# Two-operand work taken off GpSimdE in the first mixer, and half of the stacked keys of two mixers copied by DMA inside SBUF

## The chip, the cores and the metric

The kernel runs on one core of a Trainium2 chip. The metric is device time in microseconds, the median over runs of one whole execution; the time of a profiled execution is given beside it. Engines are named as in the profile: PE (TensorE), DVE (VectorE), ACT (ScalarE), POOL (GpSimdE), SP (SyncE, which issues the DMAs here).

## What is computed

The reference is one inference step of a four-layer trunk over 128 context tokens and 512 latent tokens of width 1024. Each layer has a token mixer, a residual with layer norm, and a squared-ReLU MLP of width 4096. The mixers are, in order, differential attention, neighbourhood attention, grouped-query attention and a Hyena long convolution. The change touches the first two. Of the first mixer it matters that each of its 8 heads has two score maps, and that keys and queries of latent tokens are rotated:

```
def attend(k, v):
    k1, k2 = jnp.split(k, 2, axis=-1)
    def block(qb):
        q1, q2 = jnp.split(qb, 2, axis=-1)
        p1 = softmax_f32(jnp.einsum("bqhd,bkhd->bhqk", q1, k1) * scale)
        p2 = softmax_f32(jnp.einsum("bqhd,bkhd->bhqk", q2, k2) * scale)
        return jnp.einsum("bhqk,bkhd->bqhd", (p1 - lam * p2).astype(v.dtype), v)
...
o = rms_norm(o, subln_g) * (1.0 - lam_init)
out = o.reshape(B, L, DA_HEADS * 2 * DA_DH) @ w_o
```

The second mixer has 16 heads of 64 dimensions, handled in 8 pairs, with a learned bias on a window of keys, no rotation and no head norm.

## The kernel before

All matrix products run with operands split into a high part (fp32r) and a low part (the rest), each product as three matmuls (`mm3`, lines 473 to 475). Weights come from HBM by SP into three raw buffers (line 421); ScalarE casts the high part (line 450) and VectorE subtracts for the low part (line 451) into five buffers, from which a unit of matmuls reads.

A mixer (`mixer_attn`) runs over 8 heads (or head pairs) `j`. For each, generators project queries and keys (`prep_q`, `prep_k`) and, for two heads at a time, values (`prep_v`). Their small later steps are closures in the list `stages`: in the first mixer the rotation (`rope`: four DMAs inside SBUF bring the partner rows into `sw`, line 1002; then `turn`, lines 1011 and 1012; then `rope_add`, line 1018), and in both mixers the stacking. `q_stack` writes, for each of the two halves of 64 rows, the high part of the query beside its low part; `k_stack` (lines 1030 to 1033) writes the high part of the key's 64 rows into both row halves of `hi`, and the low part into both row halves of `lo`, so that one matmul over 128 rows covers two products (`score_mm`, line 2001). Of `k_stack`'s four instructions two are ScalarE casts, one is a VectorE subtraction and one a GpSimdE subtraction.

Each head has five units: four blocks of 128 latent queries (`DaUnit`, `NaUnit`) and one of context queries (`CtxUnit`). `run_units` staggers them: scores of one unit, softmax of the one before, combination of the one before that (`da_combine`: two reciprocals, a factor, a scale of the second map on line 2110, a scale-and-add on line 2112), transposes (`transposed`, copies on lines 1055 and 1057), then the values (lines 2152 and 2193). A `Feeder` hands out projection steps between the units, so that the matmuls of head `j + 1` fill the waits of head `j`; `opening` runs what is left of them before a head's first scores. After the heads `o_turn` scales the first mixer's outputs by their norms (line 1112), transposes them and applies the gain.

The order of instructions on PE, DVE, ACT and SP is made by a scheduler from its own costs and priorities in program order; on GpSimdE the order is that of the program, by the line

```
with tc.manual_schedule(engines={mybir.EngineType.Pool}):
```

Every engine and SP's queue execute in order, and each instruction waits for its inputs.

Of the kernel before, what the change touches and what calls it, by code (L numbers as in the profile page):

```python
# [10 lines left out]
F32 = mybir.dt.float32  # L11
F32R = mybir.dt.float32r
I32 = mybir.dt.int32
AF = mybir.ActivationFunctionType
# [4 lines left out]
P = 128  # L19
# [5 lines left out]
NT = TOK // P  # L25
# [253 lines left out]
class Trunk:  # L279
# [725 lines left out]
    def rope(self, x, cs):  # L1005

        nc = self.nc
        sw = self.swapped(x, LAT)

        def turn():  # L1010
            nc.gpsimd.tensor_mul(sw, sw, cs[:, 1])
            nc.vector.tensor_mul(x, x, cs[:, 0])
            self.turned = sw

        return turn
# [10 lines left out]
    def k_stack(self, hi, lo, x, h):  # L1026

        nc = self.nc
        own, oth = slice(64 * h, 64 * h + 64), slice(64 - 64 * h, 128 - 64 * h)
        nc.scalar.copy(hi[own], x[own])  # L1030
        nc.vector.tensor_sub(lo[own], x[own], hi[own].bitcast(F32))
        nc.scalar.copy(hi[oth], x[own])
        nc.gpsimd.tensor_sub(lo[oth], x[own], hi[own].bitcast(F32))

    def split(self, hi, lo, x):
        self.nc.scalar.copy(hi, x)
        self.nc.vector.tensor_sub(lo, x, hi.bitcast(F32))
# [65 lines left out]
    def o_turn(self, o, gain, ss, norm):  # L1103

        nc = self.nc

        def root(js):
            self.rsqrt(norm[:, :, js], ss[:, :, js], 1.0 / 128)

        def scale(j):  # L1110
            ov = o[:, :, j]
            nc.gpsimd.tensor_mul(ov, ov, norm[:, :, j:j + 1].to_broadcast([P, NT, P]))

        def turn(j):
            for t0, n in ((0, 3), (3, 2)):
                ps = self.b1([P, 3, P], "ot")
                for t in range(n):
                    nc.tensor.transpose(ps[:, t], o[:, t0 + t, j], self.ident)
                nc.scalar.activation(o[:, t0:t0 + n, j], ps[:, 0:n], AF.Copy, scale=gain)

        out = []
        for j0, n in ((0, 2), (2, 2), (4, 2), (6, 1), (7, 1)):
            out.append((j0 + n, lambda js=slice(j0, j0 + n): root(js)))
            for j in range(j0, j0 + n):
                out += [(j0 + n, lambda j=j: scale(j)), (j0 + n, lambda j=j: turn(j))]
        return out
# [13 lines left out]
    def mixer_attn(self, l):  # L1140
        nc, tc, a = self.nc, self.tc, self.a
        da = l == 0
        nm = "da" if da else "na"
        with tc.tile_pool(name=f"at{l}", bufs=1) as scr:
            self.scr = scr
            if da:
                o = self.L(F32, f"o{l}").rearrange("p (t k f) -> p t k f", t=NT, k=KD)
                split = self.o_parts(lambda kh, t: o[:, t, 4 * kh:4 * kh + 4])
            else:
                o = self.L(F32, f"o{l}").rearrange("p (k t) -> p k t", k=KD)  # L1150
# [6 lines left out]
            if da:  # L1157
                room = scr.tile([P, 2, 2, LAT], F32R, name="qroom")
                cs = vv[:, 0, 6:10].rearrange("p (a c) f -> p a (c f)", a=2)
# [9 lines left out]
                norm = scr.tile([P, NT, 8], F32, name="norm")  # L1169
# [64 lines left out]
            def prep_k(j):  # L1234
                k = self.S(F32, "k32")
                kc = kc_room[:, j % 2]
                h = heads.setdefault(j, {})
                h["kc"] = kc
                h["ks"] = [[ksr[:, j % 2, i, s] for s in range(2)] for i in range(2)]
                nc.sync.dma_start(k[:, cut:cut + CTX], a[nm + "_ck"][j])  # L1240
                yield from self.project(nm, 2 * j + 1, ((kc, 0, CTX, None), (k[:, 0:cut], CTX, CTX + cut, None), (k[:, cut + CTX:], CTX + cut, TOK, None)))
                nc.sync.dma_start(self.o[nm + "_ks"][j], kc)
                if da:
                    stages.append(self.rope(k[:, 0:LAT], cs))

                def stack():
                    if da:
                        self.rope_add(k[:, 0:LAT])
                    for i in range(2):
                        self.k_stack(*h["ks"][i], k, i)  # L1250

                stages.append(stack)
                if not (da and j == 0):
                    next(ada, None)
                    yield 850
# [850 lines left out]
def da_combine(nc, e0, e1, m, neglam):  # L2106

    nc.vector.reciprocal(m[:, 4:6], m[:, 2:4])
    nc.vector.tensor_mul(m[:, 5:6], m[:, 5:6], neglam)
    nc.gpsimd.tensor_mul(e1, e1, m[:, 5:6].to_broadcast(list(e1.shape)))  # L2110
    yield
    nc.vector.scalar_tensor_tensor(out=e0, in0=e0, scalar=m[:, 4:5], in1=e1, op0=ALU.mult, op1=ALU.add)

# [6 lines left out]
class DaUnit(Unit):  # L2120
# [5 lines left out]
    def scores(self):  # L2126
        k, nc, hd = self.k, self.k.nc, self.heads[self.j]
        pss = []
        for h in range(2):
            ps = k.b2([P, 2, 512], "s")  # L2130
            self.score_mm(ps, hd, h, FULL)
            pss.append(ps)
        yield
        m = k.small(6, "m")
        es = []
        for h, ps in enumerate(pss):
            k.softmax_stats(ps[:, :, :HALF], m[:, h:h + 1])
            e = k.S(F32, "e")
            nc.scalar.activation(e.rearrange("p (a b) -> p a b", a=2), ps[:, :, :HALF], AF.Exp, bias=m[:, h:h + 1], scale=1.0, accum_out=m[:, 2 + h:3 + h])
            es.append(e)  # L2140
        yield
        yield from da_combine(nc, es[0], es[1], m, self.neglam)
        yield es[0]
# [12 lines left out]
class CtxUnit(Unit):  # L2156
# [5 lines left out]
    def scores(self):  # L2162
        k, nc, hd = self.k, self.k.nc, self.heads[self.j]
        ps = k.b1([P, 2, P], "sc")
        for h in range(2):
            nc.tensor.matmul(ps[:, h], hd["qc"][:, h * P:(h + 1) * P], hd["kc"], start=True, stop=True)
        yield
        m = k.small(6, "m")
        nc.vector.tensor_reduce(m[:, 0:2], ps, axis=AX.X, op=ALU.max, negate=True)
        e = k.S(F32, "e", 256).rearrange("p (a b) -> p a b", a=2)  # L2170
        rs = hd["rs"][:, 0] if "rs" in hd else None
        if rs is not None:
            nc.vector.tensor_mul(m[:, 0:2], m[:, 0:2], rs)
        for h in range(2):
            nc.scalar.activation(e[:, h], ps[:, h], AF.Exp, bias=m[:, h:h + 1], scale=1.0 if rs is None else rs[:, h:h + 1], accum_out=m[:, 2 + h:3 + h])
        yield
        if self.neglam is not None:
            yield from da_combine(nc, e[:, 0], e[:, 1], m, self.neglam)
        else:
            nc.vector.reciprocal(m[:, 4:6], m[:, 2:4])  # L2180
            nc.gpsimd.tensor_mul(e, e, m[:, 4:6].unsqueeze(2).to_broadcast([P, 2, P]))
            yield
        yield e
# [37 lines left out]
```

## Time and profile before

| | |
|---|---|
| Median of 3 runs | 3435.16 us (3433.51 to 3438.25) |
| Profiled execution | 3427.73 us |
| Its span | 3425.9 us |
| Granted TensorE clock, mean | 0.993 |
| PE busy | 3297.3 us (96%) |
| PE weight loads busy | 3166.2 us (92%) |
| DVE busy | 2559.7 us (75%) |
| ACT busy | 1511.8 us (44%) |
| POOL busy | 823.4 us (24%) |

The span runs from the first to the last instruction of the profiled execution. Busy shares are averages over the whole span. Matmuls overlap, and their ends are modelled, so that a busy PE can still have room. Times within the rows are microseconds from the span's start. The first mixer's heads lie between about 50 and 400 us, the second's between about 950 and 1220 us.

### The profile page before, as it was taken

What the parts mean: (1) busy time and instruction counts of PE and PEld (TensorE: products, weight loads), DVE (VectorE), ACT (ScalarE), POOL (GpSimd) and SP (SyncE); (2) the same over time, 40 slices, a digit from 0 to 9 for tenths busy, and PEclk for the clock granted to TensorE, in tenths of its full rate; (3) what the DMA queues carried; (4) which work ended last, traced back from release to release, by engine and by line L of the source; (5) the groups of instructions that cost most, each with busy time, mean ns of one, the idle gap of its engine ahead of it and who ended that gap; (6) DMA issues with size and microseconds to landing.
All of it is one profiled execution on the core that took longest, in us unless ns stands there. A gap on an engine that the chain in (4) does not pass through costs nothing.

```text
span 3425.9 us, 63752 instructions
## 1 busy us (share of the span) xinstructions
PE 3297.3 (96%) x25288; PEld 3166.2 (92%) x25288; DVE 2559.7 (75%) x4876; ACT 1511.8 (44%) x2704; POOL 823.4 (24%) x842
## 2 busy tenths in 40 slices
PE   8999899999999999999998999999999999999998
PEld 6878898999999999999997889999998998999998
DVE  4777888788586678778678878877859888845457
ACT  3555453343366654333345665333325334532322
POOL 0323213334234431123222011231321112100002
PEclk9999999999999999999999999999999999999999
DMA  7343135555332325545422112545533224322221
GB/s 275 125 129 107 66 126 162 171 163 182 95 126 79 104 73 173 186 159 196 162 73 64 31 54 99 185 160 179 168 101 121 80 83 159 107 76 75 92 75 50
DMA packets 157643, 418.96 MB, mean 122 GB/s; under 512 B 19550, under 2 KB 29414, under 8 KB 154270
## 3 DMA queue, kind: packets, MB, share of 16 engines
q1 hardware_dynamic: 157344, 414.88, 36.9%
q8 instruction: 199, 3.26, 0.4%
q14 instruction: 100, 0.82, 0.1%
HBM read 371.20 MB, written 34.05 MB: 118 GB/s over the span
## 4 chain that ended last, share of the span: by engine, by line
PE 58%; DVE 12%; issue 4%; ACT 2%; POOL 1%; DMA 1%; SPq 0%; DVEq 0%; POOLq 0%; ACTq 0%
PE w L473 14%; PE w L474 14%; PE w L475 14%; DVE hl L451 2%; PE pv L2048 1%; DVE gtmp L653 1%; PE s L2001 1%; DVE ada L541 1%; PE ptp L1051 1%; PE qk L473 1%; PE qk L475 1%; PE qk L474 1%; PE py L1764 1%; DVE r L660 1%; POOL hywork L1742 1%
## 5 line engine op out<-in xcount | busy, mean ns | idle before, releaser
L451 DVE TENSOR_TENSOR hl<-raw,hl 128x1024 fp32r<-128x1024 f32 x411 | 537.7, 1311 | 319.5 <-ACT hl L450 318.4
L450 ACT CAST hl<-raw 128x1024 fp32r<-128x1024 f32 x411 | 430.2, 1048 | 674.9 <-PE w L475 552.0
L473 PE MATMUL w<-hl,ff 128*128 128x256 f32 x2560 | 715.8, 280 | 6.9 <-DVE gtmp L653 6.6
L474 PE MATMUL w<-hl,ff 128*128 128x256 f32 x2560 | 715.4, 279 | 2.0 <-DVE hl L451 1.9
L475 PE MATMUL w<-hl,ff 128*128 128x256 f32 x2560 | 713.9, 279 | 0.0
L660 POOL TENSOR_TENSOR r<-r,gtmp 128x256 f32<-128x256 f32 x416 | 413.5, 1007 | 1185.3 <-DVE gtmp L653 1135.9
L473 PE MATMUL w<-hh,hl 128*128 128x320 f32 (+2 forms) x2048 | 635.5, 310 | 2.7 <-ACT fx L875 2.3
L474 PE MATMUL w<-hl,hl 128*128 128x320 f32 (+2 forms) x2048 | 631.9, 309 | 3.3 <-DVE hl L742 3.3
L475 PE MATMUL w<-hh,hl 128*128 128x320 f32 (+2 forms) x2048 | 631.9, 309 | 0.0
L473 PEld LDWEIGHTS w<-hl,ff 128*128 128x128 f32 x2560 | 481.0, 188 | 11.2 <-DVE gtmp L653 9.3
L474 PEld LDWEIGHTS w<-hl,ff 128*128 128x128 f32 x2560 | 481.2, 188 | 4.5 <-DVE hl L451 2.8
L475 PEld LDWEIGHTS w<-hl,ff 128*128 128x128 f32 x2560 | 479.9, 187 | 0.0
L653 DVE TENSOR_TENSOR gtmp<-w,gate 128x256 f32<-128x256 f32 x800 | 326.3, 416 | 182.1 <-PE w L475 167.8
L541 DVE SCALAR_TENSOR_TENSOR ada<-adaw,sil,ada 128x512 f32<-128x512 f32 x504 | 388.1, 802 | 91.0 <-DMA adaw<-in_ada_w 80.9
L473 PEld LDWEIGHTS w<-hh,hl 128*128 128x128 f32 x2048 | 384.2, 188 | 17.6 <-issue 8.4
L474 PEld LDWEIGHTS w<-hl,hl 128*128 128x128 f32 x2048 | 384.3, 188 | 4.1 <-DVE hl L742 4.1
L475 PEld LDWEIGHTS w<-hh,hl 128*128 128x128 f32 x2048 | 384.1, 188 | 0.8 <-issue 0.8
L875 ACT ACTIVATE fx<-w 128x640 f32<-128x640 f32 (+2 forms) x136 | 91.5, 673 | 461.2 <-PE w L475 450.6
L473 PE MATMUL qk<-hh,hl 128*128 128x320 f32 (+2 forms) x672 | 215.2, 320 | 0.8 <-DVE gtmp L653 0.5
L474 PE MATMUL qk<-hl,hl 128*128 128x320 f32 (+2 forms) x672 | 210.8, 314 | 1.7 <-DVE hl L742 1.7
L475 PE MATMUL qk<-hh,hl 128*128 128x320 f32 (+2 forms) x672 | 210.4, 313 | 0.0
L473 PE MATMUL w<-hl,oh 128*128 128x256 f32 x640 | 184.0, 288 | 9.8 <-DVE gtmp L653 5.5
(340 smaller groups left out, 6810.6 us busy)
## 6 DMA issues: line engine op xcount, KB each, us to landing
raw<-in_w SPq DMA_DIRECT2D x256, 512.0 KB
adaw<-in_ada_w SPq DMA_DIRECT2D x288, 256.0 KB
adaw<-in_ada_w SPq DMA_DIRECT2D x16, 1024.0 KB
raw<-ab_d SPq DMA_DIRECT2D x32, 512.0 KB
raw<-in_hy_in SPq DMA_DIRECT2D x24, 512.0 KB
adaw<-in_ada_s SPq DMA_DIRECT2D x8, 1024.0 KB
raw<-in_da_qk SPq DMA_DIRECT2D x16, 512.0 KB
gate<-gate_d SPq DMA_DIRECT2D x32, 256.0 KB
```

The source lines that it names most:

```text
L450: self.nc.scalar.copy(t[:, 0], raw)
L451: self.nc.vector.tensor_sub(t[:, 1], raw, t[:, 0].bitcast(F32))
L473: mm(ps, w[0], x[0], start=start, stop=False)
L474: mm(ps, w[0], x[1], start=False, stop=False)
L475: mm(ps, w[1], x[0], start=False, stop=stop)
L541: nc.vector.scalar_tensor_tensor(out=y, in0=raw[h], scalar=x, in1=y, op0=ALU.mult, op1=ALU.add)
L653: nc.vector.tensor_mul(tmp, ps, self.gate[2 * s + q // 2][:, (q % 2) * 256:(q % 2) * 256 + 256])
L660: eng.tensor_add(rv, rv, tmp)
L875: nc.scalar.activation(x, src, AF.Relu)
L1051: nc.tensor.transpose(ps[:, i * P:(i + 1) * P], pr[:, (done + i) * P:(done + i + 1) * P], self.ident)
L1742: eng.tensor_mul(pi[:, q, s], z4[:, q, s], h4[:, q, 1 - s])
L1764: mm(py[ct][:, par], yh[:, i, cc], inv[h][:, kt, s, par], start=kt == 0 and i == 0 and h == 0, stop=False)
```

## The change

In the first mixer the rotation's second multiplication goes from GpSimdE to VectorE, behind the first; the scale of the second score map and the scale of the outputs by their norms go from GpSimdE to ScalarE, which takes the factor as a per-row operand (for the outputs one instruction for each of five token tiles, in place of one for all five). In the first two mixers a new function `k_stack_copied` takes the place of `k_stack`: ScalarE and VectorE write one row half of `hi` and `lo`, and two DMAs on SP copy each to the other row half inside SBUF. The third mixer keeps `k_stack`.

```
--- before.py
+++ after.py
@@ -1008,8 +1008,8 @@
         sw = self.swapped(x, LAT)
 
         def turn():
-            nc.gpsimd.tensor_mul(sw, sw, cs[:, 1])
             nc.vector.tensor_mul(x, x, cs[:, 0])
+            nc.vector.tensor_mul(sw, sw, cs[:, 1])
             self.turned = sw
 
         return turn
@@ -1031,6 +1031,15 @@
         nc.vector.tensor_sub(lo[own], x[own], hi[own].bitcast(F32))
         nc.scalar.copy(hi[oth], x[own])
         nc.gpsimd.tensor_sub(lo[oth], x[own], hi[own].bitcast(F32))
+
+    def k_stack_copied(self, hi, lo, x, h):
+
+        nc = self.nc
+        own, oth = slice(64 * h, 64 * h + 64), slice(64 - 64 * h, 128 - 64 * h)
+        nc.scalar.copy(hi[own], x[own])
+        nc.vector.tensor_sub(lo[own], x[own], hi[own].bitcast(F32))
+        for t in (hi, lo):
+            nc.sync.dma_start(t[oth].bitcast(F32), t[own].bitcast(F32))
 
     def split(self, hi, lo, x):
         self.nc.scalar.copy(hi, x)
@@ -1108,8 +1117,8 @@
             self.rsqrt(norm[:, :, js], ss[:, :, js], 1.0 / 128)
 
         def scale(j):
-            ov = o[:, :, j]
-            nc.gpsimd.tensor_mul(ov, ov, norm[:, :, j:j + 1].to_broadcast([P, NT, P]))
+            for t in range(NT):
+                nc.scalar.activation(o[:, t, j], o[:, t, j], AF.Copy, scale=norm[:, t, j:j + 1])
 
         def turn(j):
             for t0, n in ((0, 3), (3, 2)):
@@ -1247,7 +1256,7 @@
                     if da:
                         self.rope_add(k[:, 0:LAT])
                     for i in range(2):
-                        self.k_stack(*h["ks"][i], k, i)
+                        self.k_stack_copied(*h["ks"][i], k, i)
 
                 stages.append(stack)
                 if not (da and j == 0):
@@ -2107,7 +2116,7 @@
 
     nc.vector.reciprocal(m[:, 4:6], m[:, 2:4])
     nc.vector.tensor_mul(m[:, 5:6], m[:, 5:6], neglam)
-    nc.gpsimd.tensor_mul(e1, e1, m[:, 5:6].to_broadcast(list(e1.shape)))
+    nc.scalar.activation(e1, e1, AF.Copy, scale=m[:, 5:6])
     yield
     nc.vector.scalar_tensor_tensor(out=e0, in0=e0, scalar=m[:, 4:5], in1=e1, op0=ALU.mult, op1=ALU.add)
```

## Rows read from the trace of the kernel before

**Rows 1.** busy us of each engine in two stretches; then granted clock, DMA

```profile
50.00:400.00 350.00, 320.41 (x2291) 283.19 (x2291) 259.85 (x479) 188.88 (x455) 110.97 (x79) 0.98 0.38 123
950.00:1220.00 270.00, 263.95 (x2106) 252.41 (x2105) 189.14 (x458) 172.57 (x434) 121.82 (x194) 0.99 0.33 103
```

**Rows 2.** TensorE waits, 50 to 400 us: sum, times, longest

```profile
PE pv L2193 <- DVE pt L1057: 5.3, 3, 3.8
...
PE ptp L1051 <- ACT e L2175: 0.2, 1, 0.2
```

**Rows 3.** GpSimdE's groups, 50 to 400 us: count, busy us, mean ns, idle before

```profile
L2110 POOL TENSOR_TENSOR e<-e,m 128x640 f32<-128x640 f32 x32 | 42.5, 1327 | 176.8 <-DVE m L2109 125.0 <-DVE m L2108 17.5 <-ACT vv L979 14.6
L1033 POOL TENSOR_TENSOR ks<-k,ks 64x640 fp32r<-64x640 f32 x16 | 31.4, 1962 | 11.4 <-ACT ks L1030 10.6
L1011 POOL TENSOR_TENSOR sw<-sw,vv 128x512 f32<-128x512 f32 x16 | 22.9, 1431 | 60.5 <-DMA sw<-q 57.4 <-DMA sw<-k 3.1
L1112 POOL TENSOR_TENSOR o<-o,norm 128x640 f32<-128x640 f32 x7 | 9.2, 1319 | 16.5 <-DVE norm L1138 10.5 <-DVE m L2109 6.0
```

**Rows 4.** line 2112, whole span: ns min/median/max, first and last start

```profile
L2112 DVE SCALAR_TENSOR_TENSOR e<-e,m,e x32: 857/886/2280, 87.3 to 387.9; 128x640 f32<-128x640 f32 x32
```

**Rows 5.** VectorE in order of time, near 265 us: start us, us, instruction

```profile
265.32 1.50 DVE L1134 TENSOR_SCALAR norm<-ss 128x10 int32<-128x10 int32 x1
```

**Rows 6.** GpSimdE in order of time, near 263 us

```profile
263.18 3.60 POOL L1033 TENSOR_TENSOR ks<-k,ks 64x640 fp32r<-64x640 f32 x2
```

**Rows 7.** TensorE in order of time, three places; brackets: idle before, what ended it

```profile
267.79 0.58 PE L2152 MATMUL pv<-vv,pt 128*128 128x128 f32 x1 [4.30 <-DVE pt L1057]
...
336.96 0.39 PE L475 MATMUL w<-hl,oh 128*128 128x256 f32 x1 [1.80 <-DVE oh L1037]
...
351.89 0.58 PE L2193 MATMUL pv<-vv,pt 128*128 128x128 f32 x1 [3.75 <-DVE pt L1057]
```

**Rows 8.** busy time and granted clock in two short stretches

```profile
267.10:270.50 3.40, 2.71 (x12) 2.71 (x13) 2.69 (x8) 0.80 (x2) 0.00 (x0) 0.53 0.02 5
349.00:355.80 6.80, 3.91 (x17) 3.91 (x18) 6.77 (x13) 3.21 (x7) 3.94 (x3) 0.52 0.10 39
```

**Rows 9.** line 1404, a scale by a per-row operand on ScalarE

```profile
L1404 ACT ACTIVATE tab<-rope,gqg x4: 821/830/832, 1784.6 to 1787.6; 128x640 f32<-128x640 f32 x4
```

**Rows 10.** ScalarE's groups, 50 to 400 us

```profile
L1032 ACT CAST ks<-k 64x640 fp32r<-64x640 f32 x16 | 11.6, 724 | 0.3
...
L979 ACT ACTIVATE vv<-qk,hmask 128x128 f32<-128x128 f32 x15 | 4.9, 374 | 1.8 <-PE qk L475 1.8
```

**Rows 11.** VectorE's groups, 50 to 400 us

```profile
L2112 DVE SCALAR_TENSOR_TENSOR e<-e,m,e 128x640 f32<-128x640 f32 x32 | 43.7, 1366 | 15.8 <-POOL e L2110 15.5
...
L1012 DVE TENSOR_TENSOR q<-q,vv 128x512 f32<-128x512 f32 x8 | 5.5, 688 | 4.3 <-DMA sw<-q 4.2
```

**Rows 12.** SP and then GpSimdE in order of time, near 1877 us

```profile
1874.98 2.43 SPq L1002 DMA_DIRECT2D sw<-q  x4
...
1879.07 1.58 POOL L1434 TENSOR_TENSOR sw<-sw,tab 128x640 f32<-128x640 f32 x1 [7.33 <-DMA sw<-q]
```

**Rows 13.** ScalarE and then SP in order of time, 201 to 206 us

```profile
201.38 0.42 ACT L977 COPY q<-qk 128x320 f32<-128x320 f32 x1 [0.67 <-PE qk L475]
...
205.89 0.55 SPq L1002 DMA_DIRECT2D sw<-q  x1
```

**Rows 14.** SP, GpSimdE and TensorE in order of time, 1034 to 1047 us

```profile
1037.96 10.79 SPq L421 DMA_DIRECT2D raw<-in_na_qk  x2
...
1037.58 3.87 POOL L1033 TENSOR_TENSOR ks<-k,ks 64x640 fp32r<-64x640 f32 x2 [3.44 <-issue]
...
1046.14 0.94 PE L2001 MATMUL s<-ks,qs 128*128 128x384 f32 x4
```

**Rows 15.** GpSimdE and TensorE in order of time, 236 to 243 us

```profile
237.31 4.07 POOL L1033 TENSOR_TENSOR ks<-k,ks 64x640 fp32r<-64x640 f32 x2 [2.45 <-ACT ks L1030]
...
242.21 0.39 PE L2001 MATMUL s<-ks,qroom 128*128 128x320 f32 x1 [1.12 <-DVE ks L1031]
```

More of the change, by code (lines that the diff above doesn't have):

```diff
@@ L1010, in turn @@
         def turn():
-            nc.gpsimd.tensor_mul(sw, sw, cs[:, 1])
             nc.vector.tensor_mul(x, x, cs[:, 0])
+            nc.vector.tensor_mul(sw, sw, cs[:, 1])
             self.turned = sw
@@ L1033, in k_stack, with k_stack_copied @@
         nc.gpsimd.tensor_sub(lo[oth], x[own], hi[own].bitcast(F32))
+    def k_stack_copied(self, hi, lo, x, h):
+        nc = self.nc
+        own, oth = slice(64 * h, 64 * h + 64), slice(64 - 64 * h, 128 - 64 * h)
+        nc.scalar.copy(hi[own], x[own])
+        nc.vector.tensor_sub(lo[own], x[own], hi[own].bitcast(F32))
+        for t in (hi, lo):
+            nc.sync.dma_start(t[oth].bitcast(F32), t[own].bitcast(F32))
     def split(self, hi, lo, x):
@@ L1110, in scale @@
         def scale(j):
-            ov = o[:, :, j]
-            nc.gpsimd.tensor_mul(ov, ov, norm[:, :, j:j + 1].to_broadcast([P, NT, P]))
+            for t in range(NT):
+                nc.scalar.activation(o[:, t, j], o[:, t, j], AF.Copy, scale=norm[:, t, j:j + 1])
         def turn(j):
@@ L1249, in stack @@
                     for i in range(2):
-                        self.k_stack(*h["ks"][i], k, i)
+                        self.k_stack_copied(*h["ks"][i], k, i)
                 stages.append(stack)
@@ L2109, in da_combine @@
     nc.vector.tensor_mul(m[:, 5:6], m[:, 5:6], neglam)
-    nc.gpsimd.tensor_mul(e1, e1, m[:, 5:6].to_broadcast(list(e1.shape)))
+    nc.scalar.activation(e1, e1, AF.Copy, scale=m[:, 5:6])
     yield
```

## The prediction

> **What bounds the kernel now.** I first read the busy time by stretch [rows 1]. In the first mixer (50 to 400 us) TensorE is busy 320.41 us of 350, VectorE 259.85, ScalarE 188.88, GpSimdE 110.97; in the second (950 to 1220) TensorE is busy 263.95 us of 270. So TensorE bounds both, and all that can be won is its idle time: 29.6 us in the first mixer and 6 us in the second. Whatever the edits save on other engines counts only where it shortens one of these waits.
>
> Then TensorE's waits in the first mixer [rows 2]: 21 groups, 29.2 us in all. By the engine that ended them, VectorE has 18.6 us, ScalarE 9.0, GpSimdE itself only 1.6. So GpSimdE looks innocent until one asks why VectorE was late. The two largest waits are one copy each out of the transposes (line 1057). Ahead of the first, VectorE runs a 10-column operation (line 1134) that takes 1.50 us while GpSimdE subtracts keys (line 1033) from 263.18 on [rows 5, 6]; ten columns are nowhere near 1.5 us of work. Just before it stands the scale-and-add of line 2112, near the longest of its kind, which range from 0.857 to 2.280 us for one size [rows 4]. I read this as the two engines holding each other up. TensorE then starts at 267.79 after 4.30 us of waiting [rows 7]. The same picture stands before 351.89 (3.75 us, key subtractions again) and, with a scale of line 2110 and a rope multiplication on GpSimdE, before 336.96 (1.80 us).
>
> The two long waits cost more than themselves [rows 8]: from 267.1 to 270.5 and from 349.0 to 355.8 the granted clock reads 0.53 and 0.52, its lower level of 1.2 GHz, after TensorE had stood. TensorE is busy 2.71 and 3.91 us in these stretches, about half of which the upper level would have saved: 1.4 + 2.0 = 3.3 us.
>
> **The change, part by part.** *Off GpSimdE in the first mixer* [rows 3]: 32 scales of 640 columns (42.5 us; 8 short ones of 128 columns go with them), 16 key subtractions (31.4), 16 rope multiplications (22.9), 8 scales of the output (9.2 us for the 7 in this stretch). With them it has nothing left between 50 and 400 us. None of this is TensorE's time; what it gives is the stretching of VectorE. Gain, first term: the three waits named, 4.30 + 3.75 + 1.80 = 9.85, and the clock, 3.3: 13.2 us. Bounds: nothing, if the stretching has another cause or the waits only move; above, all of VectorE's 18.6 and GpSimdE's 1.6 with the clock's 3.3, 23.5 us.
>
> *VectorE* gets 16 rope multiplications of 512 columns at 0.688 us [rows 11]: 11.0 us. It gets back at least 32 x (1.366 - 0.857) = 16.3 us on line 2112, whose mean follows from 43.7 us over 32 in the same stretch [rows 4, 11]. So it ends less loaded, and the remaining 18.6 - 9.85 = 8.7 us of waits that it ends should shrink; I take half, 4 us (between 0 and 8.7).
>
> *ScalarE* gets 32 scales of 640 columns by a per-row operand, 8 of 128 and 40 of 128 for the output (five token tiles for each of 8 heads). Nearest rows: 0.830 us for 640 columns with such an operand [rows 9], 0.374 for 128 columns [rows 10]: 26.6 + 3.0 + 15.0 = 44.6 us. The second key copy goes away, 11.6 us [rows 10]. Net +33 us, from 189 to 222 of 350. It is in order and ends 9.0 us of TensorE's waits; grown with its load these become 10.6: +1.6 us (between 0 and twice 9.0).
>
> *The stacked keys.* Each head now issues four copies of 64 rows of 640 fp32 elements (160 KB) on SP, 64 in all, where ScalarE and GpSimdE wrote the other half. SP takes 2.43 us for four such issues, 0.61 each, and a reader started 1.66 us after the last of four rope copies (80 KB each) was issued [rows 12]. So, from the start of the first key copy: the first high part is ready at 0.73 + 0.61 + 1.66 = 3.0 us (before, 1.5), the low part of that half at 0.73 + 0.81 + 0.61 + 1.66 = 3.8 (before 2.8), the last low part, with the four issues back to back, at 5.0; before, GpSimdE ended 4.07 us after it began, at about 4.9 [rows 15]. So the end is the same and the beginning 1.0 to 1.5 us later. Who waits? In heads 1, 4 and 7 of the first mixer the first scores already run behind the keys: in head 4 the last scores start at 242.21 [rows 15]. Three heads at 1.3 us: +4 us (0 to 4.5). In heads 2 and 6 the first score came 2.2 and 0.5 us after the last key, in heads 0, 3 and 5 over 9 us; these hide it. In the second mixer GpSimdE's part ends at 1041.45 and the first score starts at 1046.14 [rows 14], and the eight heads repeat this with room of 2.8 us or more, against a landing that moves by some 2 us: nothing, hidden by the projection matmuls that run between. The 16 subtractions less on GpSimdE and 11.6 us less on ScalarE there buy nothing either, since TensorE has no idle time to give back.
>
> The Trainium skill (DMA: Bandwidth & Descriptors, section "Anatomy of one DMA") speaks against this part: for copies issued through GpSimd it fits a fixed cost of about 2.0 us plus its bytes at 436 GB/s, so, as an estimate, 2.4 us for 160 KB where the row has 1.66 for smaller ones; by the page each of the three tight heads pays 0.7 us more, 2.1 us in the sum.
>
> *SP's queue* is in order. A key copy waits for the cast or the subtraction, and what SP has behind it (weights, the next rope copies) waits too; weights are fetched several units ahead, so some us there cost nothing. The other way round costs: the rope copy of 205.89 had its data at 201.80 [rows 13] but stood behind two weight loads whose buffers came free late. Of the 16 such rope copies 5 stood so, 2.6 to 7.4 us, 4.3 on average. For the five heads with little room that makes at most 5 x 5/16 x 4.3 = 6.7 us; since some of it meets room, I take +2.
>
> **Sum:** -13.2 - 4 + 1.6 + 4 + 2 = -9.6 us. The profiled execution took 3427.73 us (span 3425.9), below the runs' median of 3435.16 by 7.4 us; the difference is applied to the median: 3425.5 us.
>
> **Rivals.**
> *The whole relief arrives* (0.10): every wait that VectorE and GpSimdE end goes and the copies hide: -23.5 us, 3412. For it: line 2112 alone loses 16 us; against it: another order of ScalarE's and VectorE's work brings waits of its own. The Trainium skill (GPSIMD Engine Reference, section "Key points") says that GpSimd shares its SBUF interfaces with VectorE, to the cost of VectorE's operations with two SBUF inputs or in a two-port mode; by that rule every stretch of this kind goes with GpSimdE's work. Here the trace agrees so far: up to 2.280 us against 0.857 on two inputs.
>
> *ScalarE takes GpSimdE's place* (0.29): GpSimdE could stand idle for the norms (line 1138, 10.5 us of waiting before the output scales [rows 3]) without harm. ScalarE has the exponentials and the PSUM copies behind it. If it stands these 10.5 us and they reach TensorE, the sum is +0.9: 3436, no change. Against it: 222 us of work in 350 leave room, and the scales are handed out one by one.
>
> *VectorE's stretching has another cause* (0.03), such as waits of its own that the trace books as work: the first two terms vanish and +7.6 is left, 3443, just slower. Against it: the long ones stand where GpSimdE is busy.
>
> *Key copies stand behind weight loads* (0.18), the one that ends clearly slower: in the second mixer SP issues one load at 1037.96 and the next only near 1048.4 [rows 14], between the keys of head 2 and its scores at 1046.14. A copy queued behind the second is issued from 1048.75 on and the four land by 1048.75 + 2.43 + 1.66 = 1052.8; the first high part, enough to start, at 1051.0: TensorE stands about 5 us. This pattern stands for three heads (2, 4, 6): 15 us, plus the lower clock that followed such waits, 1.4 to 2.0 each, 5 us: -9.6 + 20 = +10.4, 3446. It decides once a copy is issued over some 3 us after the last subtraction. Against it: the keys are ready at 1042, six us before that load's buffer, so an order by readiness puts them first.
>
> **Chances.** Forecast 0.40 (-9.6) and the whole relief 0.10 make faster by over 0.2% (6.9 us, about what a measurement of this kernel can tell from no change) 0.50; within it 0.29; slower 0.18 + 0.03 = 0.21. The range is 3412 to 3445: from the whole relief up to just short of the queued copies; the forecast's own is 3418 to 3428.
>
> **What would show it.** After the change: GpSimdE without busy time between 50 and 400 us; line 2112 at 0.86 us throughout; the copies of line 1057 no longer ending waits of 4 us; TensorE's idle time there near 20 us instead of 29.6 and no stretch at the lower clock; the first scores of heads 1, 4 and 7 waiting for a DMA by a us or so; the second mixer as long as before. Wrong, if ScalarE's waits for norms end TensorE's, or if in the second mixer scores wait for DMAs.

## The result: faster by 35.7 us, and the profile after

The changed kernel takes 3400.36 us (median of 4 runs, 3398.76 to 3403.99) against 3436.1 us of the kernel before in the same series: 35.7 us less, a ratio of 0.990 with a 95% interval of 0.9888 to 0.9912. The prediction was 3425.5 us, with 3412 to 3445 as its range. The direction was right and the size much too small; even the rival in which the whole relief arrives, at 3412, was too slow. In later series, where the kernel before measured 3429 to 3433, kernels that are the changed one but for small variations were 31 to 34 us faster; a part of the 35.7 is thus the high reading of the kernel before in the first series.

The profiled execution took 3399.52 us (span 3397.7), 28.2 us less than that of before. I first looked where these 28.2 us arise. The last matmul of the first mixer's output projection starts at 438.4 us before and at 410.5 after, 27.9 us earlier; from there to the end the two traces stay some 26 to 29 us apart. So between these two executions the gain is the first mixer's alone.

Busy time by stretch of the changed kernel (stretch, length, then PE, PE weight loads, DVE, ACT and POOL, then granted clock and DMA):

```profile
50.00:400.00 350.00, 340.08 (x2505) 306.98 (x2504) 250.47 (x547) 222.64 (x531) 4.34 (x6) 0.99 0.47 142
950.00:1220.00 270.00, 263.27 (x2144) 250.30 (x2143) 169.09 (x447) 157.65 (x407) 90.06 (x182) 1.00 0.41 118
```

Against [rows 1], TensorE's idle time between 50 and 400 us fell from 29.6 to 9.9 us. The changed kernel is ahead, so its stretch holds more of the output projection; up to that projection's end the idle time is 31.0 us before and 9.9 after. VectorE is busy 9 us less although it has the rope multiplications more; ScalarE has 222.64 us, as the prediction worked out (222). GpSimdE's 4.34 us are residual additions that begin behind the heads.

TensorE's waits from 50 to 400 us of the changed kernel (sum, times, longest):

```profile
PE pv L2202 <- DVE pt L1066: 2.9, 1, 2.9
PE v L473 <- ACT q L977: 2.1, 1, 2.1
PE v L473 <- ACT vv L952: 1.4, 1, 1.4
PE s L2010 <- ACT e L2148: 1.0, 2, 0.7
PE w L473 <- DVE gtmp L653: 0.6, 1, 0.6
...
PE ada L585 <- DMA adaw<-in_ada_w: 0.4, 1, 0.4
```

Ten groups are left of the 21 of [rows 2], of which two of the larger are, before:

```profile
PE pv L2152 <- DVE pt L1057: 4.3, 1, 4.3
...
PE s L2001 <- DVE ks L1031: 2.2, 2, 1.1
```

VectorE ends 3.5 us of them (18.6 before), ScalarE 5.7 (9.0 before), GpSimdE none (1.6 before). No wait of TensorE is ended by a key copy. (Lines stand 9 further on from line 1035: 2193 became 2202, 1057 became 1066, 2112 became 2121.)

Line 2121 in the changed kernel (ns minimum/median/maximum, first and last start), which answers to [rows 4]:

```profile
L2121 DVE SCALAR_TENSOR_TENSOR e<-e,m,e x32: 864/882/889, 88.2 to 361.4; 128x640 f32<-128x640 f32 x32
```

The spread is gone: the longest is 889 ns where 2280 stood. Other VectorE instructions were spread as well, key subtractions and ten-column operations like the one of [rows 5]. So I took every group of VectorE instructions (one line, tile and shape) and added up, for those that GpSimdE ran beside, the time above the shortest of the group. I call this the stretch. From 50 us to the end of the output projection it is 45.3 us before and 0.9 us after. Line 2112 has 16 us of it before, of which some 10 stand beside the rope multiplications and nearly nothing beside the scale of line 2110.

What ScalarE and VectorE got (the changed kernel's groups, 50 to 400 us; first ScalarE's, then VectorE's):

```profile
L2119 ACT ACTIVATE e<-e,m 128x640 f32<-128x640 f32 x32 | 26.5, 829 | 6.3 <-DVE m L2118 6.1
...
L1121 ACT ACTIVATE o<-o,norm 128x128 f32<-128x128 f32 x40 | 13.1, 392 | 3.2 <-DVE norm L1147 3.2
```

```profile
L2121 DVE SCALAR_TENSOR_TENSOR e<-e,m,e 128x640 f32<-128x640 f32 x32 | 28.1, 878 | 6.7 <-ACT e L2119 6.2
...
L1012 DVE TENSOR_TENSOR sw<-sw,vv 128x512 f32<-128x512 f32 x16 | 10.9, 682 | 0.0
```

These durations are close to those of [rows 9 to 11] (829 ns for 830, 392 for 374, 682 for 688). VectorE now waits 6.2 us for ScalarE's scale, where it waited 15.5 us for GpSimdE's [rows 11]. ScalarE stands 3.2 us for the norms, not the 10.5 that GpSimdE stood [rows 3].

One long wait is left. VectorE, then TensorE of the changed kernel in order of time (start, us, instruction):

```profile
328.34 0.16 DVE L1145 TENSOR_TENSOR newt<-norm 128x10 f32<-128x10 f32 x1
328.42 0.88 DVE L2121 SCALAR_TENSOR_TENSOR e<-e,m,e 128x640 f32<-128x640 f32 x1
329.22 0.16 DVE L1146 SCALAR_TENSOR_TENSOR newt<-newt,ss 128x10 f32<-128x10 f32 x1
329.30 0.42 DVE L1066 COPY pt<-ptp 128x256 f32<-128x256 f32 x1
```

```profile
329.77 0.79 PE L2202 MATMUL pv<-vv,pt 128*128 128x128 f32 x2 [2.89 <-DVE pt L1066]
```

Nothing is stretched here, the ten-column operations take 0.16 us; VectorE is simply full (busy 5.94 of the 6 us from 327). The granted clock reads 0.68 there after TensorE has stood, as in [rows 8], and 0.55 near 281 us (stretch, length, PE, PE weight loads, DVE, ACT, POOL, clock, DMA):

```profile
327.00:333.00 6.00, 3.21 (x13) 2.91 (x14) 5.94 (x20) 4.53 (x13) 0.00 (x0) 0.68 0.42 97
281.00:284.50 3.50, 3.50 (x19) 3.50 (x18) 1.92 (x4) 1.86 (x3) 0.00 (x0) 0.55 0.39 112
```

So a wait of VectorE's own and time at the lower level (1.2 GHz) remain though GpSimdE has no work there.

### The profile page after: what moved, and what is told of

Same layout as the page of the kernel before. It is cut to its first block, busy times and chain, and to the rows that moved or that the text cites. A ratio compares the mean times of both kernels' runs of the same rounds, so it can differ in the third digit from the quotient of the medians.

```text
span 3397.7 us, 63734 instructions
## 1 busy us (share of the span) xinstructions
PE 3288.2 (97%) x25288; PEld 3162.0 (93%) x25288; DVE 2514.5 (74%) x4892; ACT 1526.1 (45%) x2752; POOL 677.2 (20%) x746
## 4 chain that ended last, share of the span: by engine, by line
PE 54%; DVE 13%; issue 4%; ACT 2%; DMA 2%; POOL 2%; SPq 0%; DVEq 0%; POOLq 0%; ACTq 0%
PE w L473 13%; PE w L474 13%; PE w L475 13%; DVE hl L451 2%; PE pv L2057 1%; DVE gtmp L653 1%; DVE ada L541 1%; PE s L2010 1%; PE ptp L1060 1%; PE qk L473 1%; DMA adaw<-in_ada_w 1%; PE qk L475 1%; PE qk L474 1%; PE py L1773 1%; DVE r L660 1%
## 5 line engine op out<-in xcount | busy, mean ns | idle before, releaser
L473 PEld LDWEIGHTS w<-hl,ff 128*128 128x128 f32 x2560 | 481.1, 188 | 11.9 <-DVE gtmp L653 10.1
```

The lines of the kernel that those rows point to most:

```text
L473: mm(ps, w[0], x[0], start=start, stop=False)
```

## The experiments

Three theories stood at the start. A: GpSimdE's two-operand work stretches VectorE's instructions, and the stretch is the loss. B: the second exponential's scale on GpSimdE was a slow link of the chain from scores to transposes. C: the copied keys give the gain. In the table, "end" is the start of the last matmul of the first mixer's output projection in the trace (us) and "stretch" is as defined above (us); differences of ends are taken before rounding; medians stand beside that of the kernel before in the same series.

| run | median, before (us) | ratio, 95% | end | stretch |
|---|---|---|---|---|
| kernel before | | | 438.4 | 45.3 |
| changed kernel | 3400.36, 3436.10 | 0.9888 to 0.9912 | 410.5 | 0.9 |
| e1_only | 3412.09, 3431.94 | 0.9921 to 0.9951 | 424.6 | 25.7 |
| rope_o_only | 3423.04, 3431.94 | 0.9955 to 0.9980 | 431.9 | 26.2 |
| k_only | 3423.85, 3431.94 | 0.9963 to 0.9984 | 435.2 | 26.0 |
| no_k | 3407.30, 3431.94 | 0.9905 to 0.9934 | 420.9 | 17.7 |
| ns15 | 3402.05, 3432.72 | 0.9894 to 0.9927 | 408.5 | 0.6 |
| dum_two | 3438.45, 3432.72 | 1.0004 to 1.0023 | 444.6 | 51.7 |
| dum_one | 3408.93, 3432.72 | 0.9913 to 0.9943 | 417.9 | 19.7 |
| dum_e | 3412.61, 3429.22 | 0.9934 to 0.9959 | 418.8 | 15.5 |
| dum_rest | 3428.12, 3429.22 | 0.9982 to 1.0001 | 435.0 | 36.3 |
| dum_act | 3404.23, 3432.49 | 0.9904 to 0.9934 | 410.5 | 0.6 |
| k_first | 3398.89, 3432.72 | 0.9884 to 0.9914 | 408.9 | 0.7 |
| gq | 3398.54, 3432.49 | 0.9883 to 0.9916 | 410.9 | 0.7 |
| hy | 3385.46, 3432.49 | 0.9846 to 0.9876 | 411.0 | 0.7 |
| gq_hy | 3379.26, 3432.49 | 0.9833 to 0.9862 | 411.6 | 0.7 |
| gq_hy_ab | 3380.62, 3429.22 | 0.9840 to 0.9867 | 408.9 | 0.6 |

### One edit at a time

e1_only is the kernel before with this edit alone:

```
-    nc.gpsimd.tensor_mul(e1, e1, m[:, 5:6].to_broadcast(list(e1.shape)))
+    nc.scalar.activation(e1, e1, AF.Copy, scale=m[:, 5:6])
```

> The kernel before with one edit, the scaling of the second exponential on ScalarE. Theory A (two-operand work on GpSimdE stretches VectorE's instructions, and the gain follows how much of it is gone): L2110 is 48 of some 116 us of such work in the first mixer, so the gain is 48/116 of 35.7, some 15 us: 3421. Theory B (GpSimdE was a slow link of the chain from scores to transposes, and only this multiplication lies on that chain): nearly the whole gain, 28 to 36 us: 3400 to 3408. Theory C (the copied keys give the gain): none, 3436.

rope_o_only has these two:

```
-            nc.gpsimd.tensor_mul(sw, sw, cs[:, 1])
             nc.vector.tensor_mul(x, x, cs[:, 0])
+            nc.vector.tensor_mul(sw, sw, cs[:, 1])
...
-            nc.gpsimd.tensor_mul(ov, ov, norm[:, :, j:j + 1].to_broadcast([P, NT, P]))
+            for t in range(NT):
+                nc.scalar.activation(o[:, t, j], o[:, t, j], AF.Copy, scale=norm[:, t, j:j + 1])
```

> The kernel before with two edits, the rotation's multiplication on VectorE and the output scaling on ScalarE. Theory A: 33 of 116 us of two-operand work go, some 10 us faster: 3426. Theory B: neither is on the chain of scores, within 3 us of before. Theory C: within 3 us of before.

k_only calls `k_stack_copied` in both mixers and changes nothing else; no_k is the changed kernel with `k_stack` in its place.

```
-                        self.k_stack(*h["ks"][i], k, i)
+                        self.k_stack_copied(*h["ks"][i], k, i)
```

> The kernel before with one edit, the copied keys in both mixers. Theory A: 33 of 116 us of two-operand work go in the first mixer, some 10 us faster, less what the copies cost: by the prediction 4 us in heads 1, 4 and 7 and 2 us in the SP queue, so 3430. Theory B: no gain and those 6 us, 3436 to 3442. Theory C: most of the gain, 3400 to 3410.

> The kernel after with the keys as before, three of the four edits. Theory A: 82 of 116 us go, some 25 us faster than before: 3411; with the prediction's 6 us for the copies it would be 3405. Theory B: 3400 or faster by the 6 us that the copies would cost, 3394 to 3400. Theory C: 3430 or slower.

Alone the edits give 19.9, 8.9 and 8.1 us by the medians; together 36.8, so they add up to the whole. no_k keeps 24.6, and theory A had put 25 there. C falls. B alone falls too: it gave the second and third edit nothing, and no_k the whole gain. But A's shares don't fit quite either: each edit takes 19 to 20 us of stretch away (their sum, 58, is more than the 44.4 of the whole change, so stretch doesn't add up), and the first gives twice as much for it.

The traces show what the other two lose. Half the length of the stretches at the lower clock, from 50 us to the end, is 6.8 us before and in e1_only, but 11.9 in rope_o_only and 10.2 in k_only; and in k_only TensorE waits 6.3 us for DMAs. The ends lie 13.8, 6.4 and 3.2 us earlier than before; without these losses they would lie, as an estimate, 13.8, 11.6 and 12.9 us earlier, so equal stretch is worth about the same.

In k_only TensorE does wait for key copies (its waits, 50 to 400 us):

```profile
PE s L2010 <- DMA ks<-ks: 3.9, 3, 1.8
```

Three waits, 3.9 us in all. That the prediction had 4 us is luck: it spread them over heads 1, 4 and 7 at 1.3 us each, and all three stand in head 7, between 344.99 and 348.92 us. The first of them ends 2.57 us after the issue of the first copy began, where the prediction had 0.61 + 1.66 = 2.27. Two more waits, 2.4 us, are for weights of line 523 that pass through the same queue and were not waited for before; whether the copies held them up is not shown. The edit still gains 8, and added to the others it gains 7 more (3407.30 to 3400.36, two series) with no such wait left.

### The work put back where nothing reads it

ns15 makes room (`NS = 16` becomes 15). dum_two adds to it multiplications of the sizes that the change took off GpSimdE, and a subtraction per key half; their result goes to a tile that nothing reads:

```
+            nc.gpsimd.tensor_mul(DUM[0][:, 0:4], DUM[1].rearrange("p (t f) -> p t f", t=NT)[:, 0:4], sw.rearrange("p (t f) -> p t f", t=4))
...
+            nc.gpsimd.tensor_mul(DUM[0], DUM[1].rearrange("p (t f) -> p t f", t=NT), norm[:, :, j:j + 1].to_broadcast([P, NT, P]))
...
+                            nc.gpsimd.tensor_sub(DUM[0].rearrange("p t f -> p (t f)")[own], k[own], h["ks"][i][0][own].bitcast(F32))
...
+    nc.gpsimd.tensor_mul(DUM[0][:, 0:n], DUM[1].rearrange("p (t f) -> p t f", t=NT)[:, 0:n], m[:, 5:6].unsqueeze(2).to_broadcast([P, n, P]))
```

dum_one has the same four places with one tensor operand:

```
+            nc.gpsimd.tensor_copy(DUM[0][:, 0:4], sw.rearrange("p (t f) -> p t f", t=4))
...
+            nc.gpsimd.tensor_scalar(out=DUM[0], in0=DUM[1].rearrange("p (t f) -> p t f", t=NT), scalar1=norm[:, 0, j:j + 1], scalar2=None, op0=ALU.mult)
...
+                            nc.gpsimd.tensor_copy(DUM[0].rearrange("p t f -> p (t f)")[own], h["ks"][i][0][own].bitcast(F32))
...
+    nc.gpsimd.tensor_scalar(out=DUM[0][:, 0:n], in0=DUM[1].rearrange("p (t f) -> p t f", t=NT)[:, 0:n], scalar1=m[:, 5:6], scalar2=None, op0=ALU.mult)
```

> The kernel after with 15 rows of scratch instead of 16; the same work. It makes the room that the next two kernels need and is what they are compared with. All theories: within 5 us of after, 3397 to 3406.

> The kernel of 15 rows with extra GpSimdE work at the places and of the sizes that the change emptied in the first mixer: two-operand multiplications and subtractions whose result nothing reads; the outputs stay those of the reference. Theory A: the stretching comes back and with it most of the loss, 20 to 36 us slower than the 15-row kernel. Theory B (slow link in the chain): nothing reads the results, so within 5 us of the 15-row kernel.

> The same extra work on GpSimdE with one tensor operand instead of two (a copy, or a multiplication by a column of factors). If it is the second operand that stretches VectorE: within 5 us of the 15-row kernel. If any work on GpSimdE does: slower by as much as with two operands, in proportion to its busy time. Theory B: within 5 us.

Unread two-operand work costs 36.4 us against ns15, the whole gain and a little more; unread one-operand work 6.9 us. GpSimdE is busy alike in both from 50 to 400 us, 118.1 and 125.1 us. This decides for A: no result is awaited, and the loss comes back. That the unread work holds buffers which others need is no rival either: from 50 to 440 us of dum_two's trace no wait of another engine or of SP is booked on an unread instruction. Nor is it another order of work: up to the end of the output projection TensorE, VectorE and ScalarE run the same instructions in the same order in ns15, dum_two, dum_one, dum_e and dum_rest. (Between the kernel before and the changed one the scheduler's order does change: of 607 VectorE instructions up to there 483 keep their place, and what that alone gives or costs was not measured.) What makes the two kinds differ is less sure. They differ in the second tensor operand, but copies also stand where subtractions stood, and another kind of instruction where the products stood; that it is the operand and not the kind of instruction is not shown. One-operand work is not free either: its stretch is 19.7 us and moves the end by 9.4 us. The loss is read in the trace of dum_two, VectorE then GpSimdE in order of time:

```profile
359.24 0.15 DVE L1148 SCALAR_TENSOR_TENSOR newt<-newt,ss 128x10 f32<-128x10 f32 x1
359.31 0.41 DVE L1067 COPY pt<-ptp 128x256 f32<-128x256 f32 x1
359.65 1.33 DVE L1149 SCALAR_TENSOR_TENSOR norm<-newt,norm 128x10 f32<-128x10 f32 x1
360.90 0.81 DVE L1041 TENSOR_TENSOR ks<-k,ks 64x640 fp32r<-64x640 f32 x1
361.63 1.51 DVE L1147 TENSOR_TENSOR newt<-norm 128x10 f32<-128x10 f32 x1
```

```profile
359.42 3.70 POOL L1265 TENSOR_TENSOR dum<-k,ks 64x640 f32<-64x640 f32 x2 [2.42 <-issue]
```

Ten columns take 1.33 and 1.51 us while the unread subtractions run, 0.15 just before. What follows on TensorE shows in the busy times and clock of the same kernel:

```profile
358.70:368.90 10.20, 7.66 (x29) 6.32 (x30) 10.14 (x18) 5.03 (x12) 6.46 (x4) 0.51 0.30 64
```

VectorE is full, TensorE idles 2.5 of 10.2 us, and the clock is granted at 0.51. Up to the end of the output projection the clock takes 17.1 us in dum_two and 1.7 in ns15 (half the length of the stretches at the lower level), of the 36.2 us by which their ends differ; TensorE's idle time grows from 9.6 to 31.9. In the profiled execution of before the clock took 6.8 us, in that of the changed kernel 5.1.

One-operand work stretches the scale-and-add (line 2132) less; dum_two first, then dum_one:

```profile
L2132 DVE SCALAR_TENSOR_TENSOR e<-e,m,e x32: 858/881/2202, 90.1 to 395.8; 128x640 f32<-128x640 f32 x32
```

```profile
L2132 DVE SCALAR_TENSOR_TENSOR e<-e,m,e x32: 858/884/1430, 89.5 to 368.7; 128x640 f32<-128x640 f32 x32
```

The single edits had left the first one's double gain open. dum_e puts back only its unread multiplication, dum_rest only the others.

> The kernel of 15 rows with only the 40 two-operand multiplications of the second exponential's size put back on GpSimdE, their product read by nothing. If stretch at that place is all that the edit took away: some 20 us slower than the 15-row kernel, 3422. If half of that edit's 19.8 us came from the slow link in the chain: some 10 us slower, 3412.

> The kernel of 15 rows with the other GpSimdE work put back unread (rotation, key subtraction, output scaling) and not the second exponential's. If stretch is all: 16 us slower than the 15-row kernel, 3418, as the single edits gave 8.9 and 8.1. If unread work at those places costs more because ScalarE and VectorE are fuller in the changed kernel: 20 to 26 us slower.

By the medians dum_e costs 14 us more than ns15 and dum_rest 30 (differences to before, 16.6 and 1.1 against 30.7; two series). So stretch makes most of the first edit's 19.9 us. Nor need the rest be the slow link: dum_e has 14.9 us of stretch, where e1_only took 19.6 away, and in both the end moves by 0.70 us for each us (10.4 and 13.8 us). The others cost more put back than their removal had given; 13.7 of the 26.6 us by which dum_rest ends later than ns15 are clock (15.4 against 1.7). No wait of another engine or of SP is booked on an unread instruction in dum_rest's trace from 50 to 440 us either. In the traces the ends move by 0.6 to 0.75 us for each us of stretch in the four pairs with the cleanest difference: before to changed kernel 27.9 for 44.4, ns15 to dum_e 10.4 for 14.9, to dum_rest 26.6 for 35.7, to dum_two 36.2 for 51.1. The other pairs lie lower where clock or DMA waits come in: before to rope_o_only 0.34, to k_only 0.17; and ns15 to dum_one, 0.49.

### ScalarE's room

dum_act adds to ns15 a ScalarE scale of the second exponential's size behind each of the 40, unread:

```
     nc.scalar.activation(e1, e1, AF.Copy, scale=m[:, 5:6])
+    n = e1.shape[1]
+    nc.scalar.activation(DUM[0][:, 0:n], DUM[1][:, 0:n], AF.Copy, scale=m[:, 5:6])
```

> The kernel of 15 rows with one more ScalarE instruction of the size of L2119 behind each of its 40 (some 31 us in the first mixer) whose result nothing reads. If ScalarE is near its limit there (the prediction's rival, ScalarE takes GpSimdE's place): 10 to 30 us slower than the 15-row kernel. If ScalarE has slack, as the after trace reads (its waits fell): within 6 us, 3402 to 3408.

Its group from 50 to 400 us, then the busy times of that stretch:

```profile
L2125 ACT ACTIVATE dum<-vv,m 128x640 f32<-128x640 f32 (+1 forms) x40 | 29.5, 737 | 0.0
```

```profile
50.00:400.00 350.00, 339.73 (x2507) 305.52 (x2506) 250.33 (x549) 245.61 (x571) 4.34 (x6) 1.00 0.47 142
```

29.5 us more on ScalarE cost 2 us, within what the runs differ (the scheduler's order differs a little from that of ns15 here). ScalarE has room; the rival in which it takes GpSimdE's place is out.

### The copied keys in the second mixer

k_first chooses `k_stack_copied` where `da` is true and `k_stack` elsewhere.

> The kernel after with the copied keys in the first mixer only; the second mixer as before. All theories hold the first mixer at what after has. The prediction put the second mixer's part at 0 (rival: 10 us lost behind weight loads): 3400 by the prediction, 3390 by that rival; if the relief of GpSimdE there helped, it is slower than after.

3398.89 us: no difference to the changed kernel that these runs can tell. The second mixer's scores last 231.5 us before (987.2 to 1218.7) and 230.4 after. There the copies neither give nor cost.

### The same cause further on

gq makes edits of these kinds in the third mixer (the rotation in two places), hy moves the fourth mixer's filter products, gq_hy has both, gq_hy_ab also the filter taps' subtractions:

```
-                nc.gpsimd.tensor_mul(sw, sw, t[1])
+                nc.vector.tensor_mul(sw, sw, t[1])
...
-                    self.k_stack(kk[:, i, h, 0, 0:LAT], kk[:, i, h, 1, 0:LAT], x[:, CTX:], h)
+                    self.k_stack_copied(kk[:, i, h, 0, 0:LAT], kk[:, i, h, 1, 0:LAT], x[:, CTX:], h)
...
-            nc.gpsimd.tensor_mul(e, e, m[:, 4:6].unsqueeze(2).to_broadcast([P, 2, P]))
+            for h in range(2):
+                nc.scalar.activation(e[:, h], e[:, h], AF.Copy, scale=m[:, 4 + h:5 + h])
```

```
-                    eng = nc.vector if q * s else nc.gpsimd
+                    eng = nc.vector
...
-            nc.gpsimd.tensor_sub(v[:, 256:512], win[:, 0:256], win[:, 256:512])
+            nc.vector.tensor_sub(v[:, 256:512], win[:, 0:256], win[:, 256:512])
```

> The kernel after with the same four kinds of edit in the third mixer, which idles TensorE 17.2 us and loses 3.4 us of clock: the rotation's multiplications on VectorE, the keys' other half by DMA, the two-head scaling of the context unit on ScalarE (that one acts in the second mixer too). Theory A: VectorE's stretch there is 20.2 us under GpSimdE work, against 44 in the first mixer, so at the first mixer's rate 10 to 16 us less; but half of GpSimdE's work there (residuals) stays, so 3 to 10 us: 3391 to 3398. If third-mixer idle time has other causes (its long wait of 5.4 us is at its start): within 3 us of after.

> The kernel after with the 48 products of the fourth mixer's filter that ran on GpSimdE on VectorE. VectorE there is stretched 13 us by them and gains 48 instructions of 0.415 us, 20 us. Theory A with VectorE as the limit there: 3 to 10 us slower. If the stretch is on the path and the added work is not: up to 10 us faster.

> Both of the edits before together: their sum, whichever signs they have; 3388 to 3408.

> The kernel with the third and fourth mixer relieved, and the 40 subtractions of the filter taps (during the first mixer's feed-forward part) on VectorE too. VectorE is stretched 11 us by them and gains 40 of 0.4 us, 16 us; TensorE idles 15.0 us between 400 and 960 us, 5.6 of it for VectorE's line 541. Stretch on the path: 3 to 6 us faster than without it, 3374. VectorE's load the limit: 2 to 5 us slower.

gq alone shows nothing: 3398.54 us, which is its second case, that third-mixer idle time has other causes. hy gives 13 us against gq in the same series and 15 against the changed kernel in the first, more than either case that I had written down. Line 1752, the 1024-column product beside them, in the changed kernel and in hy:

```profile
L1752 DVE TENSOR_TENSOR hywork<-hywork,hs x16: 1217/1759/1765, 2599.2 to 2874.4; 128x1024 f32<-128x1024 f32 x16
```

```profile
L1752 DVE TENSOR_TENSOR hywork<-hywork,hs x16: 1216/1222/1226, 2600.1 to 2861.5; 128x1024 f32<-128x1024 f32 x16
```

VectorE does 48 products more and its busy time from 2554 to 2930 us grows by only 13 us (325.64 to 338.61), though hy is ahead there and the stretch holds more of what follows. TensorE's largest wait of that mixer in the changed kernel was booked on ScalarE:

```profile
PE py L1773 <- ACT yy L1757: 12.3, 14, 1.2
```

In hy 0.4 us of it are left: ScalarE had only been the last link behind VectorE's and GpSimdE's work. hy does not part stretch from a slow link, as VectorE also waited 5.8 us for GpSimdE's products in the changed kernel (line 1754 for line 1751). Both edits together make the fastest kernel of the study, 3379.26 us, 53 us below the kernel before and faster than the 3388 to 3408 expected; the taps add nothing to it, where 3374 or a loss was expected.

## Why the prediction was right in kind and wrong in size

*The mechanism* held. GpSimdE has no work in the heads, line 2112's spread is gone, the copies of line 1057 end no wait of 4 us, and dum_two brings it all back. The Trainium skill (SBUF — State Buffer, section "Who interferes with whom") says that a VectorE instruction with two SBUF inputs contends with a GpSimd instruction that reads SBUF, and that a reduction never does; the trace agrees on the first, in the spread of line 2132 above, and with the second in line 1050 of the last section, which reads PSUM besides, so that the two can't be told apart. The Trainium skill (the same page, section "SBUF: two separate sides") also says that whichever comes second blocks for the whole instruction. For one-operand work this case's trace differs: beside such multiplications line 2132 in dum_one loses 2.5 us in 19.6 us of overlap, 0.57 us at most, while one of 640 columns takes 1.83 us.

*The step that failed is the sum:* it priced the relief by VectorE's waits and some clock, and set 7.6 us of costs against it. It gave a gain of 9.6 us for the profiled execution, and up to the end of the output projection it was 27.9. The missing 18.3 us are these:

- The cost terms, 7.6 us, did not come: ScalarE +1.6, key copies +4, SP's queue +2.
- Waits that other engines ended had no place among the gains. ScalarE's fell from 9.0 to 5.7 us and GpSimdE's from 1.6 to nothing, 4.9 together.
- VectorE's waits fell by 15.1 us where the sum had 13.9. That part was nearly right, 1.2 short.
- TensorE is busy 6.8 us less, where the sum had 3.3 for the clock: 3.5 more.
- Other idle time, most of it behind 400 us, fell by 1.5; against it stands a DMA wait of 0.4.

Why ScalarE's waits fell shows in dum_two: unread GpSimdE work gives ScalarE nothing to do, and yet, in the same order of instructions, TensorE's waits that end with ScalarE grow from 5.3 us in ns15 to 15.7 (50 to 400 us). ScalarE itself then waits longer for VectorE: 30.1 us for its copies of the outputs, 18.6 in ns15 (50 to 440 us).

The prediction's opening, that only TensorE's idle time can be won, was wrong: from 50 us to the end of the output projection TensorE is busy 357.4 of 388.4 us before and 350.6 of 360.5 after. Idle time makes 21.1 us of the 27.9, busy time 6.8, for the same matmuls. The clock term itself gave nothing: the two stretches at the lower level that it counted (3.4 and 6.8 us long) are gone, but two of the same lengths stand at 281 and 329 us after the change. 1.7 us come from one of 3.4 us at 55.7 us before, which has no successor; the other 5 I did not trace further.

*Of the costs,* the key copies' waits came in k_only and not in the full change. In head 4 the four copies are issued from 229.45 to 232.20 and the first score starts at 232.35 without a wait for a DMA; no score in any tight head waited for one. SP's queue does stand at the copies: at the first one of each head it waits for ScalarE's cast, 32.1 us in the eight heads and 8.1 at most, and what is behind it waits too. But the only wait of TensorE for a DMA from 50 to 400 us is 0.4 us long, for weights.

*The step from the profile to the median* failed as well. The profiled execution of before lay 7.4 us under its median, and I carried that over; that of after lies 0.8 under its own. These 7.5 us are the rest between 28.2 and 35.7. Part of it is the first series: in the later ones the median of before lies only 1.5 to 5.0 us above the profiled execution. Part may be the clock: the later runs of before were granted a mean of 0.991 to 0.994 (0.993 in the profiled one), those after 0.994 or 0.995, and the runs of before at 0.991 took 3.7 us more on average than those at 0.993. That the change took such lower-clock stretches away in the runs that were not profiled is not shown.

*The rivals.* The whole relief was the nearest, and short by 11.6 us for the reasons above. ScalarE in GpSimdE's place fell with dum_act and with the 3.2 us that it stands for the norms, another cause of the stretch with dum_two, copies behind weight loads with k_first and the unchanged second mixer. *Of the signs named,* TensorE's idle time was to be near 20 us and is 9.9; no stretch at the lower clock was to remain, and two did, near 281 and 329 us.

## What to carry to other kernels

When an engine's instructions of one shape spread over two to one in the trace, add up the whole spread and price that, not only the waits that the profile books on the engine: here each us of stretch on VectorE cost 0.6 to 0.75 us at the end in the clean pairs, and 0.17 to 0.5 where something else came in, through waits booked on ScalarE and through the clock too. A price of this kind is no constant. Two-operand work on GpSimdE beside a VectorE that feeds TensorE is worth moving even onto VectorE itself: it paid in hy, where VectorE had been busy for 87% of the fourth mixer (2554 to 2930 us of the changed kernel). A cost found for one edit alone (the key copies' 3.9 us) need not come back in the full change, as it did not here; and compare the clock of several runs, not of one profile, before carrying a difference over.

## What the runs showed of the hardware

The VectorE instructions looked at that read PSUM are not stretched. In dum_two, the row maximum of line 1050 and the copy of line 1067, which both read PSUM, run as ever beside the same GpSimdE work:

```profile
L1050 DVE TENSOR_REDUCE m<-s x128: 796/816/826, 77.9 to 2050.7; 128x1 f32<-128x640 f32 x128
```

```profile
L1067 DVE COPY pt<-ptp x120: 277/418/426, 93.1 to 2060.8; 128x256 f32<-128x256 f32 x112, 128x128 f32<-128x128 f32 x8
```

From 50 to 400 us 23 of line 1050 run beside GpSimdE, for 13.5 us; they take 813 ns on average, the 41 others 815. Over all VectorE instructions that overlap GpSimdE's two-operand work there, 109.3 us of overlap hold 49.8 us of stretch; in dum_one it is 9.0 of 78.1 beside multiplications with one operand and 9.9 of 32.1 beside copies. So a copy stretches VectorE by more, for its time, than such a multiplication does.

A multiplication is not faster on GpSimdE with one tensor operand, and a copy is faster than a subtraction. The unread product of 640 columns with a broadcast column as second tensor and the subtraction of keys in dum_two, then the product with a column of factors and the copy of keys in dum_one (50 to 400 us):

```profile
L2130 POOL TENSOR_TENSOR dum<-vv,m 128x640 f32<-128x640 f32 (+1 forms) x40 | 49.8, 1244 | 178.5 <-DVE m L2127 168.2 <-DVE m L2126 7.5 <-DVE newt L1147 2.4
L1265 POOL TENSOR_TENSOR dum<-k,ks 64x640 f32<-64x640 f32 x16 | 31.0, 1936 | 6.6 <-issue 4.9 <-ACT ks L1040 0.7
```

```profile
L2130 POOL TENSOR_SCALAR dum<-vv,m 128x640 f32<-128x640 f32 (+1 forms) x40 | 73.3, 1832 | 157.9 <-DVE m L2127 145.0 <-DVE m L2126 9.9 <-DVE newt L1147 1.8
...
L1265 POOL COPY dum<-ks 64x640 f32<-64x640 f32 x16 | 18.9, 1179 | 4.3 <-ACT ks L1040 3.4
```

One issue of a key copy (SP, changed kernel) takes 0.468 us at the median, one of a rope copy of half the size (kernel before) 0.582. The prediction's 0.61 us is the spacing of four issues in a row:

```profile
L1042 SPq DMA_DIRECT2D ks<-ks x64: 461/468/557, 62.2 to 1160.5; - x64
```

```profile
L1002 SPq DMA_DIRECT2D sw<-q x64: 507/582/1097, 51.9 to 1981.1; - x64
```
